# Two-part eviction straight from the banks, low parts and squares from GpSimd to VectorE, and tokens added in the banks, in a four-layer transformer on one core

## Chip, core and metric

The kernel runs on one core of a Trainium2 chip. A core has TensorE (PE, matmuls and transposes), VectorE (DVE), ScalarE (ACT), GpSimd (POOL) and SyncE (SP, which issues DMAs). Matmul results land in PSUM, eight banks of 128 partitions x 512 fp32; all else is in SBUF. The metric is the device time of one execution in microseconds (us), as the median over runs; lower is better. All times below are in us unless marked ns.

## The reference

256 tokens of width 1024 pass two blocks. The first block has two layers, each of a mixer, a feed-forward and a gated per-layer input:

```python
h = h + mix(_rms(h, norm_mix[i]))            # i=0: moba + dilated attention; i=1: compressed/selected/window attention (nsa)
h = h + _swiglu(_rms(h, norm_ffn[i]), w_ffn_gate[i], w_ffn_up[i], w_ffn_down[i])
gate = jax.nn.sigmoid(_rms(h, norm_ple[i]) @ w_ple_gate[i])
h = h + gate * (p[i] @ w_ple_proj[i])
```

The second block has two layers, each of a hybrid mixer (windowed attention beside a short convolution) and a mixture of 32 experts with two experts per token, and a last norm:

```python
x = x + hybrid_mixer(rmsnorm(x, norm_mix[l]), ...)
x = x + hierarchical_moe(rmsnorm(x, norm_ffn[l]), ...)
return rmsnorm(x, norm_final)
```

## The kernel before

**Numbers in two parts.** Most matrix products are made to fp32 accuracy from fp32r operands: an operand is cast to a high part, and its low part is the difference. `mm3` (L329 to L331) then issues three matmuls: high x high, low x high, high x low. In the first block and in the hybrid mixers, weights and activations are both split so. In the expert stages the weights go through TensorE unsplit.

**Weights.** SP loads weight blocks of 1 MB into a ring of SBUF buffers. `Split` turns them into parts, in the order of a job list: `make` casts the high part on ACT (L193) and puts the low part on a list, and `lows` issues the listed subtractions (L201) on `self.second`, which is DVE, but POOL during the per-layer gate (`ple`, L921) and at the transition into the second hybrid layer. `get(job)` casts what is needed, then as many further jobs as buffers allow (`pump`, unless `ahead` is false), then issues all the low parts, and hands out the job's parts. All engines work through their own queues in program order, so the place of a call in the program sets the order on ACT and DVE.

**Normalisation.** `Norm.half` squares half a token tile (ACT, with the sum accumulated), and POOL scales the first half's sum (L344). `norm` makes the reciprocal root (`rs`, DVE and ACT) and writes the normalised tile `xn` on DVE (L352). `turn(t)` transposes it by eight TensorE transposes of 128 x 128 (L366), four into each of two banks. Then, before the change, ACT scales bank 0's four chunks by the gain back into `xn` (L378), with a cast of two chunks into the high parts XH behind each pair (L373); DVE scales bank 1's four chunks (L382); ACT casts those in one instruction of 512 columns; DVE makes the low parts XL by three subtractions (L386). There are two token tiles, t = 0 and 1, and one turn for each before every stage.

**First block.** `last_steps` (L870) stands at the end of each mixer: the output projection's finish with the next norm, two products with the per-layer input's projection (`ple_product`, copied from their banks by ACT, L868), then `turn(0)` and `turn(1)` for the feed-forward, in an order written by hand in the list T1. `ffn` runs over 22 blocks of the hidden width: gate and up matmuls into one bank, silu on ACT (L903), product on DVE (L904), cast and difference (L905, L906), and the down matmuls of the block before. `ple` runs over two token tiles, two output halves and four weight blocks each; the sigmoid is L943, its product with the saved projection L946, the addition to the residual stream h L390; the next stage's `turn(0)` stands inside its second tile. The second layer's attention is planned by `Attention`, with the projections (`proj_steps`) stepped through beside it.

**Second block.** The hybrid mixers sum squares of their outputs in `halves`, with the additions on POOL (L1350). An expert layer runs over 16 pairs of experts; each pair's result is scattered back onto the tokens by matmuls (L1795) that accumulate in four banks `total` over all pairs. `Router.take` had replaced the tokens in h by a high and a low part; at the last pair, `join` (L1532) adds them into h again, on DVE and POOL, and `add_tiles` then adds the banks to h. After the first expert layer this is the transition into the second hybrid layer, where it is interleaved with weight casts; after the second, the tail: squares, reciprocal root, scaling by the final gain (L1863) and four output DMAs (L1864) from temporary buffers.

Of the kernel before, what the change touches and what calls it, by code (L numbers as in the profile page):

```python
# [153 lines left out]
class Split:  # L154


    def __init__(self, nc, ring, size):
        self.nc, self.ring, self.size = nc, ring, size
        self.jobs, self.at, self.made, self.free, self.low, self.pools = [], {}, {}, [], [], []
        self.second = nc.vector  # L160
        self.spare = 1

# [35 lines left out]
    def lows(self):  # L198

        for eng, vl, src, vh, key in self.low:  # L200
# [3 lines left out]
        self.low = []  # L204
# [56 lines left out]
def tile_kernel(ctx: ExitStack, tc: tile.TileContext, x, out, cat, sat, stop=None):  # L261
# [71 lines left out]
    class Norm:  # L333
# [12 lines left out]

        def norm(self, t):
# [13 lines left out]
        def turn(self, t, raw=False):  # L361
            src = h[:, t] if raw else self.xn[t]
            xn = tmp.tile([128, D], F32, name="xn", tag="xn") if raw else self.xn[t]
# [3 lines left out]

            to = [self.to[:, t, k] if self.low is None else xn[:, 128 * k:128 * k + 128] for k in range(8)]
            f_ = [slice(128 * c, 128 * c + 128) for c in range(4)]

            def parts(a, b):
                v = xn[:, 128 * a:128 * b].rearrange("p (c n) -> p c n", n=128)
                nc.scalar.copy(self.to[:, t, a:b], v)  # L373
                return self.low[:, t, a:b], v, self.to[:, t, a:b]

            lows = []
# [106 lines left out]
    with ExitStack() as c1:  # L483
# [83 lines left out]
        def proj(name, b, nq, pair=None, skew=None, mid=None, bank=acc, ahead=True):  # L567
# [30 lines left out]
            yield 0, o[0]  # L598
# [265 lines left out]
        def ple_product(i, b, pp, pv):  # L864

            for t, o in proj(f"pp{i}", b, 1, pp, bank=wps, ahead=False):
# [3 lines left out]
        def last_steps(i, outp, nxt, pp, pv):  # L870
            fns = [lambda: outp.finish(nxt, T1[10 + 6 * i]), lambda: ple_product(i, 0, pp, pv), lambda: ple_product(i, 1, pp, pv),
                   lambda: nxt.turn(0), lambda: nxt.turn(1)]
            for k in sorted(range(len(fns)), key=lambda k: T1[11 + 6 * i + k]):
                fns[k]()
# [46 lines left out]
        def ple(i, nm, pv, nxt):  # L921

            seq = [(b, q) for b in range(2) for q in range(4)]
            split.second = nc.gpsimd
# [24 lines left out]
            split.second = nc.vector  # L949
# [149 lines left out]
        def nsa(nm, nxt):  # L1099
# [142 lines left out]
            att.hold()  # L1242
            next(fill)
# [3 lines left out]
            att.run(AT1)  # L1247
            side.drain()
# [20 lines left out]
    with ExitStack() as c2:  # L1269
# [41 lines left out]
        def mixer(l, qkv, sq, yh, yl):  # L1311
# [31 lines left out]
            def halves(br, c, y, gain, n):  # L1343
# [166 lines left out]
        class Router:  # L1510
# [19 lines left out]
            def join(self, t, eng):  # L1530

                eng.tensor_add(self.tokens[:, t], self.high[:, t], self.low[:, t])  # L1532
# [147 lines left out]
        def moe(l, nm, rt, after, until):  # L1680
# [111 lines left out]
            def scatter(pr, ys, back, n):  # L1792
                for t in range(2):
# [29 lines left out]
            for pr in range(16):  # L1823
# [24 lines left out]
            for n in range(2):  # L1848
# [108 lines left out]
```

## Time and profile before

| | us |
|---|---|
| median of 3 runs | 1916.67 (1911.02 to 1917.64) |
| the profiled execution | 1910.32 |
| its span, first to last instruction | 1908.5 |
| TensorE / DVE / ACT / POOL busy | 1777.5 / 811.0 / 674.4 / 69.1 |
| mean granted TensorE clock, share of full | 0.974 |

The stages follow each other: first layer's mixer 0 to 141, feed-forward to 332, gate to 370, second layer's mixer to 534, feed-forward to 724, gate to 763, hybrid mixer to 862, experts to 1318, hybrid mixer to 1460, experts to 1897, tail to 1908.5. A duration in a row is that of one instruction or of the run of instructions that the row counts; instructions of one engine overlap a little at their ends, so that the distance of two starts is shorter than a duration. The bracket gives the engine's idle time just before, and what ended it.

### The profile page before, as it was taken

The numbers are of one execution on the slowest core, as the hardware profiler recorded it, in microseconds if no ns is written. First come the engines' busy times: TensorE is split into PE (matmuls) and PEld (weight loads), VectorE is DVE, ScalarE is ACT, GpSimd is POOL, SyncE is SP. The second block draws the span as 40 slices with busy tenths as digits, with TensorE's granted clock in tenths as the row PEclk, the third lists the DMA queues.
The fourth block names the chain that finished last, engine by engine and source line by source line (L and its number), as shares of the span: only waits on it lengthen the run. The fifth ranks groups of instructions, "written<-read, shape, count | busy, mean of one in ns | idle before, by whom it ended". The sixth has DMA issues, their size and how long they took to land. (4 is left out here: it accounts for less than half of the span.)

```text
span 1908.5 us, 25241 instructions
## 1 busy us (share of the span) xinstructions
PE 1777.5 (93%) x9983; PEld 1169.5 (61%) x9983; DVE 811.0 (42%) x1772; ACT 674.4 (35%) x1371; POOL 69.1 (4%) x92
## 2 busy tenths in 40 slices
PE   8998999898999999999999978997999999978996
PEld 6778999786689997874444443443874444433442
DVE  6667455767775556872111111113773111111112
ACT  6656445646574446651111110113552111110111
POOL 0000000300000003000000000001010000000000
PEclk9999999999999999999999989998998999998998
DMA  8437555442255554749999999999649999999996
GB/s 299 154 125 244 203 188 193 131 160 66 95 177 199 199 191 134 267 164 396 421 421 421 420 421 378 422 420 385 223 155 374 420 421 421 420 420 377 421 421 279
DMA packets 152908, 555.76 MB, mean 291 GB/s; under 512 B 9872, under 2 KB 69712, under 8 KB 103632
## 3 DMA queue, kind: packets, MB, share of 16 engines
q1 hardware_dynamic: 150672, 546.45, 73.9%
q0 software_dynamic: 2112, 7.63, 1.2%
q8 instruction: 81, 1.33, 0.3%
q14 instruction: 43, 0.35, 0.1%
HBM read 552.96 MB, written 1.09 MB: 290 GB/s over the span
## 5 line engine op out<-in xcount | busy, mean ns | idle before, releaser
L1745 PE MATMUL wps<-wring,h 128*64 128x512 f32 x1936 | 454.0, 596 | 10.6 <-DMA wring<-in_w_expert_up_dram 7.9
L1745 PEld LDWEIGHTS wps<-wring,h 128*64 128x64 f32 x1936 | 150.0, 138 | 287.3 <-issue 258.6
L201 DVE TENSOR_TENSOR wlo<-wring,whi 128x1024 fp32r<-128x1024 f32 (+1 forms) x273 | 288.3, 1094 | 73.6 <-ACT whi L193 73.3
L193 ACT CAST whi<-wring 128x1024 fp32r<-128x1024 f32 (+1 forms) x283 | 254.8, 945 | 23.0 <-PE acc L331 12.0
L329 PE MATMUL wps<-xh,whi 128*128 128x256 f32 x832 | 236.5, 284 | 4.7 <-ACT xh L373 4.7
L330 PE MATMUL wps<-xl,whi 128*128 128x256 f32 x832 | 234.8, 282 | 1.3 <-DVE xl L386 1.3
L331 PE MATMUL wps<-xh,wlo 128*128 128x256 f32 x832 | 234.5, 282 | 0.0
L1780 PE MATMUL wps<-wring,aT 128*64 128x512 f32 x984 | 227.4, 597 | 0.0
L1758 DVE SCALAR_TENSOR_TENSOR a<-wps,gs,a 128x256 f32<-128x256 f32 x64 | 28.0, 479 | 369.8 <-PE wps L1745 369.8
L329 PEld LDWEIGHTS wps<-xh,whi 128*128 128x128 f32 x832 | 157.5, 189 | 10.5 <-ACT xh L373 5.2
L1789 DVE SCALAR_TENSOR_TENSOR yl<-wps,gs,yh 128x512 fp32r<-128x512 f32 x64 | 47.9, 750 | 267.8 <-ACT yh L1788 263.9
L331 PEld LDWEIGHTS wps<-xh,wlo 128*128 128x128 f32 x832 | 160.3, 193 | 0.0
L330 PEld LDWEIGHTS wps<-xl,whi 128*128 128x128 f32 x832 | 157.5, 189 | 3.2 <-DVE xl L386 1.8
L329 PE MATMUL acc<-whi,xh 128*128 128x512 f32 (+1 forms) x360 | 146.6, 407 | 3.3 <-ACT whi L193 3.3
L1780 PEld LDWEIGHTS wps<-wring,aT 128*64 128x64 f32 x984 | 70.8, 137 | 128.4 <-issue 123.0
L331 PE MATMUL acc<-whi,xl 128*128 128x512 f32 (+1 forms) x360 | 141.3, 392 | 8.5 <-DVE xl L386 8.5
L330 PE MATMUL acc<-wlo,xh 128*128 128x512 f32 (+1 forms) x360 | 141.4, 393 | 2.3 <-DVE wlo L201 2.3
L1788 ACT ACTIVATE yh<-wps,gs 128x512 fp32r<-128x512 f32 x64 | 43.8, 687 | 262.9 <-PE wps L1780 212.2
L1769 ACT COPY aT<-wps 128x256 f32<-128x256 f32 x32 | 11.9, 372 | 239.7 <-PE wps L1768 239.7
L1755 ACT ACTIVATE a<-wps,gs 128x512 f32<-128x512 f32 x32 | 22.0, 688 | 179.9 <-PE wps L1745 179.9
L331 PEld LDWEIGHTS acc<-whi,xl 128*128 128x128 f32 x360 | 69.8, 194 | 24.9 <-DVE xl L386 10.2
L329 PEld LDWEIGHTS acc<-whi,xh 128*128 128x128 f32 x360 | 70.1, 195 | 18.1 <-ACT whi L193 4.6
(374 smaller groups left out, 2424.5 us busy)
## 6 DMA issues: line engine op xcount, KB each, us to landing
wring<-in_w_expert_down_dram SPq DMA_DIRECT2D x123, 1024.0 KB, 19.8
wring<-in_w_expert_up_dram SPq DMA_DIRECT2D x122, 1024.0 KB, 19.8
wring<-in_w_expert_gate_dram SPq DMA_DIRECT2D x120, 1024.0 KB, 19.8
wring<-in_w_ffn_gate_dram SPq DMA_DIRECT2D x22, 1024.0 KB, 9.1
wring<-in_w_ffn_up_dram SPq DMA_DIRECT2D x22, 1024.0 KB, 5.4
wring<-in_w_ffn_down_dram SPq DMA_DIRECT2D x22, 1024.0 KB, 7.4
wring<-in_w_in_dram SPq DMA_DIRECT2D x18, 1024.0 KB, 8.6
wring<-in_w_in_ab_dram SPq DMA_DIRECT2D x10, 1024.0 KB, 8.7
```

Source lines behind the costliest of these rows:

```text
L193: self.nc.scalar.copy(vh, src)
L201: eng.tensor_sub(vl, src, vh)
L329: nc.tensor.matmul(o, lh, rh, start=start, stop=False)
L330: nc.tensor.matmul(o, lh, rl, start=False, stop=False)
L331: nc.tensor.matmul(o, ll, rh, start=False, stop=stop)
L1745: nc.tensor.matmul(o[i][64 * ab:64 * ab + 64, :], xg[:, k, at:at + 64], ws[ab][:, c, :], start=k == 0, stop=k == 7)
L1755: nc.scalar.activation(a, o[0], AF.Silu, scale=r)
L1758: nc.vector.scalar_tensor_tensor(a[:, s_], o[1][:, s_], r, a[:, s_], ALU.mult, ALU.mult)
L1769: (nc.vector.tensor_copy if hf else nc.scalar.copy)(aT[:, 2 * hf:2 * hf + 2], pt[:, 256 * hf:256 * hf + 256].rearrange("p (j n) -> p j n", ...
L1780: nc.tensor.matmul(y[d2][64 * ab:64 * ab + 64, :], aT[:, 2 * hf + j, 64 * ab:64 * ab + 64], ws[ab][:, j, 512 * d2:512 * d2 + 512], start=h ...
L1788: nc.scalar.activation(ys[0][:, s_], y[d2], AF.Copy, scale=g)
L1789: nc.vector.scalar_tensor_tensor(ys[1][:, s_], y[d2], g, ys[0][:, s_], ALU.mult, ALU.subtract)
```

## The change

- `turn`: for each of the eight chunks, ACT scales it from its bank straight into the high part, and DVE makes the low part by one instruction that scales the same chunk of the same bank and subtracts the high part. The casts, the subtractions and the detour over `xn` go.
- `last_steps`: `turn(0)` moves between the two pieces of the last product.
- `ple` and the transition: low parts stay on DVE. The transition takes its tiles by `take`: squares from the banks, copies to h and the sum's offset on DVE, and only the first low part ahead of `turn(0)`.
- `Split.late`, set in the second attention: the low parts of jobs cast ahead are issued at the next `get`.
- `halves`: the additions of squares go to DVE.
- Experts: `join` goes; at pair 14, eight matmuls with an identity add the tokens' high and low parts in the banks.
- Tail: scatter by token tile, squares from the banks, gain product on DVE, last scaling half on ACT and half on DVE, output from h.

```diff
@@ class Split
     def make(self, spare=0):
...
+        if key not in self.ring.tiles:
+            self.lows()
...
-    def lows(self):
-
-        for eng, vl, src, vh, key in self.low:
+    def lows(self, n=None):
+
+        now, self.low = self.low[:n], [] if n is None else self.low[n:]
+        for eng, vl, src, vh, key in now:
             eng.tensor_sub(vl, src, vh)
...
     def get(self, job, ahead=True):
...
+        n = len(self.low) if self.late else None
         if ahead:
             self.pump()
-        self.lows()
+        self.lows(n)
@@ class Norm
+        def banks(self, t, v):
+
+            junk = tmp.tile([128, 512], BF16, name="junk", tag="junk", bufs=1)
+            s0, s1 = (small.tile([128, 1], F32, name="ss", tag=f"ss{t}{b}", bufs=2) for b in range(2))
+            for b, s in enumerate((s0, s1)):
+                nc.scalar.activation(junk, v[b], AF.Square, accum_out=s)
+            self.ss[t, 0], self.ss[t, 1] = s0, s1
+
+        def offset(self, t):
+            nc.vector.tensor_scalar(self.ss[t, 0], self.ss[t, 0], 1.0 / D, EPS, ALU.mult, ALU.add)
@@ def turn
-            for c in range(4):
-                nc.scalar.activation(to[c], pts[0][:, f_[c]], AF.Copy, scale=self.gain[:, c:c + 1])
-                if c % 2 and self.low is not None:
-                    lows.append(parts(c - 1, c + 1))
-            for c in range(4):
-                nc.vector.tensor_scalar(to[4 + c], pts[1][:, f_[c]], self.gain[:, 4 + c:5 + c], None, ALU.mult)
-            if self.low is not None:
-                lows.append(parts(4, 8))
-            for o, v, hi in lows:
-                nc.vector.tensor_sub(o, v, hi)
+            for c in range(8):
+                v = pts[c // 4][:, 128 * (c % 4):128 * (c % 4) + 128]
+                g, to = self.gain[:, c:c + 1], self.to[:, t, c]
+                if self.low is not None:
+                    nc.scalar.activation(to, v, AF.Copy, scale=g)
+                    nc.vector.scalar_tensor_tensor(self.low[:, t, c], v, g, to, ALU.mult, ALU.subtract)
...
@@ def proj
+                    if between and t == 0:
+                        yield 0, o[0]
+                        between()
@@ def last_steps
+            outp.finish(nxt, T1[10 + 6 * i])
+            ple_product(i, 1 - i, pp, pv)
+            ple_product(i, i, pp, pv, lambda: nxt.turn(0))
+            nxt.turn(1)
@@ def ple
-            split.second = nc.gpsimd
@@ second attention
+            split.late = True
             next(fill)
             for _ in att.start():
...
             att.run(AT1)
+            split.late = False
@@ def halves
-                    nc.gpsimd.tensor_add(sq[:, br], sq[:, br], s_)
+                    nc.vector.tensor_add(sq[:, br], sq[:, br], s_)
@@ experts
-                if pr == 15:
+                if pr == 14:
+
+                    idr = ptile([128, 128], F32R, "idr", bufs=1)
+                    nc.scalar.copy(idr, ident)
                     for t in range(2):
-                        rt.join(t, nc.gpsimd if t else nc.vector)
+                        for d2 in range(2):
+                            for part in (rt.high, rt.low):
+                                nc.tensor.matmul(total[t][d2], idr, part[:, t, :, 64 * d2:64 * d2 + 64].rearrange("p k q -> p q k"),
+                                                 start=False, stop=False, skip_group_check=True)
@@ tail
-            for n in range(2):
-                scatter(*last, n)
+            for t in range(2):
+                for n in range(2):
+                    scatter(*last, n, (t,))
...
+            for t in range(2):
+                after.banks(t, total[t])
             for t in range(2):
                 for b in range(2):
-                    add_half(t, b, total[t][b], after)
+                    nc.vector.tensor_mul(h[:, t, bs[b]], total[t][b], nf[:, bs[b]])
+                after.offset(t)
             for t in range(2):
                 r = rs(after.ss[t, 1], 1.0 / D, 1, bias=after.ss[t, 0])
-                for b in range(2):
-                    s_ = slice(512 * b, 512 * b + 512)
-                    o = tmp.tile([128, 512], F32, name="o", tag="xn")
-                    nc.vector.scalar_tensor_tensor(o, h[:, t, s_], r, nf[:, s_], ALU.mult, ALU.mult)
-                    nc.sync.dma_start(out[0, 128 * t:128 * t + 128, s_], o)
+                nc.scalar.activation(h[:, t, bs[0]], h[:, t, bs[0]], AF.Copy, scale=r)
+                nc.sync.dma_start(out[0, 128 * t:128 * t + 128, bs[0]], h[:, t, bs[0]])
+                nc.vector.tensor_scalar(h[:, t, bs[1]], h[:, t, bs[1]], r, None, ALU.mult)
+                nc.sync.dma_start(out[0, 128 * t:128 * t + 128, bs[1]], h[:, t, bs[1]])
@@ transition
-                            add_tiles((0,), total, nm)
-                            split2.second = nc.gpsimd
+                            def take(t):
+
+                                nm.banks(t, total[t])
+                                for b in range(2):
+                                    nc.vector.tensor_copy(h[:, t, 512 * b:512 * b + 512], total[t][b])
+                                nm.offset(t)
+                                nm.norm(t)
+
+                            take(0)
                             split2.pump(PUMP[0])
+                            split2.lows(1)
+                            nm.turn(0)
                             split2.lows()
-                            nm.turn(0)
                             split2.pump(PUMP[1])
                             split2.lows()
-                            add_tiles((1,), total, nm)
-                            split2.second = nc.vector
+                            take(1)
```

## Rows read from the trace of the kernel before

**Rows 1.** The page's busy time, share of the span and instructions per engine.

```profile
PE 1777.5 (93%) x9983; PEld 1169.5 (61%) x9983; DVE 811.0 (42%) x1772; ACT 674.4 (35%) x1371; POOL 69.1 (4%) x92
```

**Rows 2.** Stretches: length, each engine's busy time, granted clock, DMA share, GB/s.

```profile
141.00:332.00 191.00, 185.41 (x1335) 174.57 (x1334) 110.36 (x145) 96.77 (x140) 2.44 (x4) 1.00 0.61 207
...
862.00:1318.00 456.00, 427.07 (x2070) 187.40 (x2069) 73.08 (x163) 60.87 (x111) 2.40 (x1) 0.97 1.00 413
```

**Rows 3.** TensorE's timeline, 139 to 166: start, duration, line, [idle before <- ended by].

```profile
145.20 0.38 PE L329 MATMUL wps<-xh,whi 128*128 128x256 f32 x1 [2.34 <-ACT xh L373]
146.34 0.39 PE L330 MATMUL wps<-xl,whi 128*128 128x256 f32 x1 [0.75 <-DVE xl L386]
...
159.88 0.50 PE L329 MATMUL acc<-whi,ah 128*128 128x512 f32 x1 [2.50 <-ACT ah L905]
```

**Rows 4.** ACT's timeline of the same stretch.

```profile
141.64 0.63 ACT L378 ACTIVATE xn<-wps,sm 128x128 f32<-128x128 f32 x2
...
146.54 9.63 ACT L193 CAST whi<-wring 128x1024 fp32r<-128x1024 f32 x10
...
159.43 0.40 ACT L905 CAST ah<-a 128x256 fp32r<-128x256 f32 x1 [1.56 <-DVE a L904]
```

**Rows 5.** DVE's timeline of the same stretch.

```profile
147.62 11.44 DVE L201 TENSOR_TENSOR wlo<-wring,whi 128x1024 fp32r<-128x1024 f32 x10 [0.26 <-ACT whi L193]
158.98 0.41 DVE L904 TENSOR_TENSOR a<-sg,wps 128x256 f32<-128x256 f32 x1
```

**Rows 6.** Timelines: DVE and ACT at 381, TensorE at 884.

```profile
381.37 0.69 DVE L1069 COPY c2k<-wps 64x508 f32<-64x508 f32 x1 [1.06 <-ACT c2k L1067]
...
380.76 1.07 ACT L1067 COPY c2k<-wps 64x512 f32<-64x512 f32 x2 [1.70 <-PE wps L1065]
...
884.84 0.50 PE L1768 MATMUL wps<-idg,a 128*128 128x128 f32 x2 [0.46 <-ACT aT L1769]
```

**Rows 7.** Two DVE lines by form: duration min/median/max in ns, first and last start.

```profile
L1758 DVE SCALAR_TENSOR_TENSOR a<-wps,gs,a x64: 473/476/486, 883.3 to 1884.5; 128x256 f32<-128x256 f32 x64
...
L1789 DVE SCALAR_TENSOR_TENSOR yl<-wps,gs,yh x64: 741/751/752, 892.3 to 1895.0; 128x512 fp32r<-128x512 f32 x64
```

**Rows 8.** TensorE's timeline at the start.

```profile
9.50 0.80 PE L329 MATMUL acc<-whi,xh 128*128 128x512 f32 x1 [2.81 <-ACT whi L193]
```

**Rows 9.** Timelines of POOL, TensorE, ACT around the gate stages; DVE lines by form.

```profile
351.48 10.65 POOL L201 TENSOR_TENSOR wlo<-wring,whi 128x1024 fp32r<-128x1024 f32 x4 [4.18 <-DVE xn L352]
...
362.46 0.50 PE L331 MATMUL acc<-whi,xl 128*128 128x512 f32 x1 [3.20 <-DVE xl L386]
...
369.40 1.11 PE L366 MATMUL wps<-idg,xn 128*128 128x128 f32 x8 [1.40 <-DVE xn L352]
...
763.80 0.63 ACT L378 ACTIVATE xn<-wps,idg 128x128 f32<-128x128 f32 x2 [5.19 <-PE wps L366]
...
L946 DVE TENSOR_TENSOR sgp<-sgp,pv x8: 678/694/1874, 341.2 to 755.8; 128x512 f32<-128x512 f32 x8
...
L390 DVE TENSOR_TENSOR h<-h,sgp x8: 691/692/2776, 341.9 to 756.5; 128x512 f32<-128x512 f32 x8
...
L386 DVE TENSOR_TENSOR xl<-xn,xh x48: 411/425/2885, 7.8 to 1339.1; 128x256 fp32r<-128x256 f32 x32, 128x512 fp32r<-128x512 f32 x16
```

**Rows 10.** DVE's timeline in the second attention.

```profile
444.18 1.23 DVE L201 TENSOR_TENSOR wlo<-wring,whi 128x1024 fp32r<-128x1024 f32 x1 [2.10 <-ACT whi L193]
```

**Rows 11.** TensorE's timeline: strided matmuls, a wait for weights, last scatter.

```profile
384.71 3.66 PE L1076 MATMUL wps<-c2k,wring 128*128 128x80 f32 x25
...
1291.35 3.65 PE L1745 MATMUL wps<-wring,h 128*64 128x512 f32 x16 [1.33 <-DMA wring<-in_w_expert_gate_dram]
...
1316.83 1.10 PE L1795 MATMUL acc<-yl,back 128*128 128x512 f32 x4
```

**Rows 12.** Timelines: TensorE at the transition, DVE at the end.

```profile
1321.25 0.63 PE L366 MATMUL wps<-idg,xn 128*128 128x128 f32 x4 [3.32 <-DVE xn L352]
...
1904.01 1.42 DVE L1863 SCALAR_TENSOR_TENSOR o<-h,rs,X 128x512 f32<-128x512 f32 x2 [0.68 <-DMA out_dram<-o]
```

More of the change, by code (lines that the diff above doesn't have):

```diff
@@ L161, in __init__ @@
         self.spare = 1
+        self.late = False
     def add(self, job, key, view, last):
@@ L203, in lows @@
                 self.ring.done(key)
-        self.low = []
     def pump(self, most=99):
@@ L362, in turn @@
             src = h[:, t] if raw else self.xn[t]
-            xn = tmp.tile([128, D], F32, name="xn", tag="xn") if raw else self.xn[t]
             pts = [wps(), wps()]
@@ L366, in turn @@
                 nc.tensor.transpose(pts[k // 4][:, 128 * (k % 4):128 * (k % 4) + 128], src[:, 128 * k:128 * k + 128], ident)
[L368 to L376, printed above, removed]
-            for c in range(4):
-                nc.scalar.activation(to[c], pts[0][:, f_[c]], AF.Copy, scale=self.gain[:, c:c + 1])
-                if c % 2 and self.low is not None:
-                    lows.append(parts(c - 1, c + 1))
-            for c in range(4):
-                nc.vector.tensor_scalar(to[4 + c], pts[1][:, f_[c]], self.gain[:, 4 + c:5 + c], None, ALU.mult)
-            if self.low is not None:
-                lows.append(parts(4, 8))
-            for o, v, hi in lows:
-                nc.vector.tensor_sub(o, v, hi)
+            for c in range(8):
[4 more added lines that the diff above has]
+                    nc.vector.scalar_tensor_tensor(self.low[:, t, c], v, g, to, ALU.mult, ALU.subtract)
+                elif c < 4:
+                    nc.scalar.activation(to, v, AF.Copy, scale=g)
+                else:
+                    nc.vector.tensor_scalar(to, v, g, None, ALU.mult)
     def add_half(t, b, v, nxt):
@@ L564, in tile_kernel, with proj @@
             plan_moe(l)
-        def proj(name, b, nq, pair=None, skew=None, mid=None, bank=acc, ahead=True):
+        def proj(name, b, nq, pair=None, skew=None, mid=None, bank=acc, ahead=True, between=None):
             o = [bank(), bank()]
@@ L595, in proj @@
                     piece(q, t)
+                    if between and t == 0:
+                        yield 0, o[0]
+                        between()
                 split.done((name, b, q))
                 side.tick()
-            yield 0, o[0]
+            if not between:
+                yield 0, o[0]
             yield 1, o[1]
@@ L862, in ple_inputs, with ple_product @@
                 yield 0
-        def ple_product(i, b, pp, pv):
-            for t, o in proj(f"pp{i}", b, 1, pp, bank=wps, ahead=False):
+        def ple_product(i, b, pp, pv, between=None):
+            for t, o in proj(f"pp{i}", b, 1, pp, bank=wps, ahead=False, between=between):
                 pv[b, t] = keep.tile([128, 512], F32, name="pv", tag="pv", bufs=4)
@@ L870, in last_steps @@
         def last_steps(i, outp, nxt, pp, pv):
[L871 to L874, printed above, removed]
+            outp.finish(nxt, T1[10 + 6 * i])
+            ple_product(i, 1 - i, pp, pv)
+            ple_product(i, i, pp, pv, lambda: nxt.turn(0))
+            nxt.turn(1)
         def ffn(i, nm, nxt):
@@ L948, in ple @@
                 nxt.norm(t)
-            split.second = nc.vector
         rows_d = dram.tile([24, 383], F32, name="rows_d")
@@ L1528, in take @@
                     nc.scalar.copy(self.high[:, t, :, s_], self.tokens[:, t, :, s_])
-            def join(self, t, eng):
-                eng.tensor_add(self.tokens[:, t], self.high[:, t], self.low[:, t])
             def turn(self, t, hf):
@@ L1790, in down, with scatter @@
                 return ys
-            def scatter(pr, ys, back, n):
-                for t in range(2):
+            def scatter(pr, ys, back, n, ts=(0, 1)):
+                for t in ts:
                     for d2 in range(2):
```

6 lines of the change are left out of this document (4 added, 2 removed).

## The prediction

> **What bounds the kernel now.** I read the page's busy table first: TensorE is busy 93% of the span, VectorE (DVE) 42%, ScalarE (ACT) 35%, GpSimd (POOL) 4% [rows 1]. So 69 us of POOL work is not a bound by its size; what counts is who waits for it, and whom it slows. The stretches come next [rows 2]. In the feed-forward stretch TensorE is busy 185 of 191 us with DMA at 0.61: what is lost or won there moves everything behind it. In an expert stretch DMA is at 1.00: a TensorE microsecond there is free as long as it is smaller than a wait for weights. So every step is priced at the idle time of TensorE around it, outside the expert stretches.
>
> At the entry of a feed-forward stage, TensorE turns both token tiles in one run of transposes, waits 2.34 for the first high part and 0.75 for the first low part, and then 2.50 more before the first down matmul at 159.88 [rows 3]. Behind the turn, ACT makes ten casts from 146.54 on, and only then the silu [rows 4]; DVE makes the ten low parts, 1.14 us apart, and only then the product at 158.98 that the down matmul needs [rows 5]. So this wait counts from the moment when ACT is through with the turn.
>
> **The new eviction.** Before, ACT scales the four chunks of one bank while DVE scales the four of the other; casts and subtractions follow in SBUF. ACT starts at 141.64 [rows 4] and, by two turns in the 4.9 us up to 146.54, needs some 2.5 a turn. After, ACT and DVE read each chunk from the same bank, one behind the other. Does ACT's next chunk wait for DVE's read? The trace of before has few pairs to ask. On the bank at 380.76, ACT copies partitions 0 to 63 and DVE partitions 64 to 127, with no data in common; DVE starts at 381.37, after 1.06 of waiting for ACT [rows 6]. TensorE, too, waits 0.46 to write one half of a bank until ACT has read the other half [rows 6]. No two engines' accesses to one bank overlap anywhere that I looked. I take it that the two readers alternate.
>
> The Trainium skill ("PSUM — Partial Sum Buffer", section "PSUM bank collisions raise a hardware error") asks for exactly this guard between engines, two readers included, in a bank and its 32-partition quadrant; by it the time is that of this forecast, and without it that of the first rival below. The trace goes further than the page, since its two readers had different quadrants and one waited all the same.
>
> One chunk then takes ACT's 0.37 (two in a row span 0.63 [rows 4]), a hand-over of some 0.04 (DVE's 158.98 plus 0.41 [rows 5], to ACT's cast of that product at 159.43 [rows 4]), DVE's read and a hand-over back. DVE's instruction is bounded below by ACT's pace for a plain scaling of the same columns, 0.31 [rows 4], and above by DVE's own two-tensor form at 256 columns, 0.476; that form at 512 columns takes 0.751 [rows 7], so a column costs 1.07 ns and 128 of them 0.34, which I take. The cycle is 0.79 (0.92 at the upper end). Eight cycles, less one overlap of some 0.4 where the bank changes, keep ACT for 5.4 instead of 2.5: **2.8 us more of ACT per turn** (2.2 to 4).
>
> **Part by part,** against the profiled execution's 1910.3:
>
> Start: the first cast of a weight stands behind the turn on ACT, and TensorE's first matmul waits 2.81 for that cast, until 9.50 [rows 8]. +2.9, the turn and a hand-over (-0.4 if the readers overlap, +4 at the slow cycle).
>
> Feed-forward entries: two, of one pattern. Turn 0 moves between two pieces of the last projection and starts some 1.2 earlier, at 140.4; two turns then take 2 x 5.4 and a copy of 0.6 between them, so the ten casts start near 152.0 instead of 146.54. The casts, ten low parts and the product shift rigidly. TensorE does not catch that up: it would finish the second gate and up blocks near 162 and wait until 165.3 instead of 159.88. +5.4 each, +10.8 (gain of 0.75 each if nothing serialises; 7 each at the upper cycle).
>
> Low parts of the per-layer gate (two stages): POOL's four in a row take 10.65, and beside them a DVE multiply takes 1.87 where the median is 0.69, an add 2.78 where it is 0.69, and a subtraction of the turn 2.89 where the wide ones take some 0.7 [rows 9]. So 5.5 us of DVE time come back when POOL is empty, against five low parts of 1.14 [rows 5], 5.7, that DVE now makes: even. What decides is ACT, whose sigmoid for the last half stands behind the serial turn. That turn ends 2.8 later by itself, and by some 2.1 more because a turn earlier in the stage was late by 2.8 and waited 0.7 less for TensorE; behind it, multiply, add and normalisation get 1.8 back from the empty POOL. So the last transposes, which TensorE waits 1.40 for before 369.40 [rows 9], come 3.0 later: +3.0. In the second layer ACT idles 5.19 before the turn there [rows 9]; less the normalisation and the transposes, some 2 in all, 3 of it is cover, of a chain that is 4.6 later, since its earlier turns are later too: +1.5. Ends: -4.3 and -5.8 if readers overlap (TensorE's wait of 3.20 at 362.46 for a subtraction beside POOL [rows 9] and its like of 3.86 in the second layer go, with some 1.1 and 1.9 of matmuls stretched behind them), +5 and +4 at the slow cycle.
>
> Delayed low parts in the second attention: three of them, like the one at 444.18 that makes DVE idle 2.10 [rows 10] with the score work of the attention queued behind it. DVE gets to that work earlier; what waits next is the cast itself. 4.85 us of DVE idle time, about half of it on the path: -2.5 (0 to -4).
>
> Squares of the other mixer: 12 additions of 256 columns leave POOL for DVE, where 256 columns take 0.41 [rows 5], so 2.5 a layer. They lie beside attention matmuls in stretches where DVE has room, and only the last pair is near the path; without the cover 0.8 a layer. 0 (-1 to +1).
>
> Tokens added in the banks: eight more matmuls of 512 columns per expert layer. Four contiguous ones last 1.10 in a row [rows 11], the last with its full length, so some 0.235 apart; 8 of them make 1.9. Their moving operand steps by 512 bytes. Of strides, the trace has 80 columns at 64 bytes, twenty-five matmuls in 3.66, 0.146 each [rows 11], and transposes at 8 bytes, 128 columns each in some 0.24 [rows 6]; the latter, carried to 512 columns, would make 0.96 each and 7.7 in all, the upper end. I take 1.9, since the row with the longer stride is the nearer. TensorE waits 1.33 for weights there, one of three such waits [rows 11], 3.9 in all, which hides 1.9 and not 7.7. 0; if the cover were gone, +1.9 a layer. The join of POOL and DVE that goes was waited for by nobody before the stage's end.
>
> The Trainium skill ("SBUF — State Buffer", section "Door 1: The DMA port swizzle") says that each access which crosses into a new 16-byte line pays a penalty; every element would do so here. By it the eight would lie toward their upper end and the sum come to the 1940 of the last rival; the row at 64 bytes, which crosses a line at each element too, does not show it.
>
> Transition: TensorE idles 3.32 before the transposes of 1321.25 [rows 12]. DVE's add (0.69 [rows 9]) no longer stands ahead of the squares, and no POOL runs beside the normalisation, about 0.9 by the slow forms of rows 9: -1.6. The turn costs 2.8, and DVE now makes four low parts of half size, 0.6 each, around it, some of which the weights' first use waits for: +0.8. +2.0 (-2 to +4).
>
> Tail: the wait of 0.68 for an output buffer goes, and ACT takes one of the last two scalings, 0.71 [rows 12]; a tile's offset no longer goes through POOL, 0.3. The load of the final gain is issued on SP ahead of the last scatter instead of behind it, with no output queued there yet. -1.7 (-0.7 to -2.1).
>
> Sum: 2.9 + 10.8 + 3.0 + 1.5 - 2.5 + 2.0 - 1.7 = **+16.0**, 1926.3 for an execution like the profiled one. The median of the runs shown is 6.4 above that execution; on it I predict **1932**.
>
> **Rivals.** *The readers overlap.* Then a turn takes 2.9 and ACT and DVE are both freed by the casts and subtractions. For it: every data dependence of the new form allows it. Against: rows 6. Terms: -0.4 at the start, -1.5 at the feed-forward entries, -1.4 at the gate stages' entries, -4.3 and -5.8 behind them, -2.5, -2.0, -2.1: -20.0, 1897. It decides at once, in every turn.
>
> *They alternate, but the cost is covered.* A projection takes a chunk in three matmuls of 0.235, 0.7, nearly the pace of 0.79, and its first low part comes after 0.8 instead of 1.8. If the ten casts weren't what the down matmul waits for, the entries would cost 2 each and the gate stages nothing: 2.9 + 4 - 2.5 - 1.7 = +2.7, 1919. Against: the order of rows 4 and 5.
>
> *The strided matmuls are slow.* 7.7 less a cover of 3.9, twice, on top of the forecast: +7.6, 1940. Against: the row at 64 bytes.
>
> **How the numbers follow.** Forecast 0.58, overlap 0.20, covered 0.16, slow strides 0.06. About 0.5% (9.6 us) is what a measurement of this kernel tells from no change. Overlap is faster; covered is mostly the same, with 0.03 faster; of the forecast 0.03 falls within 0.5%. Faster 0.23, same 0.16, slower 0.61. The forecast's own range is 1921 to 1944, which takes in all but the outermost of the ends above; reaching down over the covered case to 1905 leaves out the overlap alone, 2 in 10.
>
> **What would show it.** Right: ACT's scalings 0.79 apart with DVE's reads between them; the ten casts at the feed-forward entry starting about 10 us after TensorE's first transpose there, and an idle TensorE of over 4 us before the first down matmul; POOL nearly empty. Wrong: scalings 0.31 apart with DVE one chunk behind; casts at the old distance; the eight strided matmuls longer than 3.9; no DVE idle time saved in the second attention.

## The result and the profile after

| | before | changed |
|---|---|---|
| median, us | 1913.85 (1910.89 to 1917.64, 4 runs) | 1933.74 (1929.30 to 1934.18, 4 runs) |
| the profiled execution, us | 1910.32 | 1934.18 |
| span, us | 1908.5 | 1932.4 |

The ratio of the changed kernel to the one before is 1.0103, with a 95% interval of 1.0086 to 1.0121: slower by 1.0%, 19.9 us between the medians and 23.9 between the profiled executions. 1932 was forecast.

The page's busy table of the changed kernel, as in [rows 1]:

```profile
PE 1795.9 (93%) x9999; PEld 1179.8 (61%) x9999; DVE 810.0 (42%) x1814; ACT 679.1 (35%) x1391; POOL 21.4 (1%) x60
```

POOL is nearly empty, as was meant, and ACT and DVE are as busy as before. The loss is in their waits. Two rows of the changed kernel's view of waits (who waited for whom: us in total, times, longest):

```profile
DVE xl L386 <- ACT xh L385: 50.8, 101, 6.2
...
ACT xh L385 <- DVE xl L386: 47.3, 96, 1.7
```

L385 and L386 are the two halves of the new eviction. DVE's wait for ACT's high part is a data dependence. ACT's wait for DVE has no data in it: ACT's next chunk has nothing to do with the low part that DVE makes. 96 times are six in each of the 16 turns, one for each pair of neighbouring chunks that share a bank; 47.3 over 16 turns is 2.96 a turn.

The entry of the first feed-forward, ACT's timeline of the changed kernel (start, duration, what, idle before), answers to [rows 4]:

```profile
145.44 0.37 ACT L385 ACTIVATE xh<-wps,sm 128x128 fp32r<-128x128 f32 x1 [0.46 <-DVE xl L386]
146.23 0.37 ACT L385 ACTIVATE xh<-wps,sm 128x128 fp32r<-128x128 f32 x1 [0.42 <-DVE xl L386]
147.02 0.63 ACT L385 ACTIVATE xh<-wps,sm 128x128 fp32r<-128x128 f32 x2 [0.42 <-DVE xl L386]
...
155.64 9.59 ACT L196 CAST whi<-wring 128x1024 fp32r<-128x1024 f32 x10
```

The scalings stand 0.79 apart, with one pair 0.26 apart where the bank changes (the row with x2). The ten casts begin at 155.64. DVE and TensorE of the same stretch answer to [rows 5] and [rows 3]:

```profile
146.63 0.35 DVE L386 SCALAR_TENSOR_TENSOR xl<-wps,sm,xh 128x128 fp32r<-128x128 f32 x1 [0.44 <-ACT xh L385]
...
156.70 11.44 DVE L205 TENSOR_TENSOR wlo<-wring,whi 128x1024 fp32r<-128x1024 f32 x10 [0.58 <-ACT whi L196]
168.06 0.41 DVE L912 TENSOR_TENSOR a<-sg,wps 128x256 f32<-128x256 f32 x1
```

```profile
147.83 0.66 PE L380 MATMUL wps<-idg,xn 128*128 128x128 f32 x4 [1.02 <-DVE xl L386]
150.81 0.38 PE L333 MATMUL wps<-xh,whi 128*128 128x256 f32 x1 [2.32 <-ACT xh L385]
157.98 0.38 PE L335 MATMUL wps<-xh,wlo 128*128 128x256 f32 x1 [0.76 <-DVE wlo L205]
168.97 0.80 PE L333 MATMUL acc<-whi,ah 128*128 128x512 f32 x1 [2.76 <-ACT ah L913]
```

The first down matmul stands at 168.97 instead of 159.88. Even the transposes of the second tile are late: they wait 1.02 for DVE to leave a bank.

**Where it is lost.** The table says by how much a matmul of TensorE starts later than the same matmul (the n-th of its source line) of the kernel before, as the median over the matmuls of a stretch, from the two timelines. The columns after the first are experiments, told below. Times of the stretches are those of the kernel before.

| stretch | changed | e12 order alone | e2 old turn | e3 new turn alone | e1 alternate | e5 few casts |
|---|---|---|---|---|---|---|
| first projection, 24 to 29 | 2.7 | 0.3 | 0.1 | 2.6 | 0.9 | 2.7 |
| first attention's end, 115 to 128 | 4.4 | 1.8 | 0.0 | 4.2 | 2.4 | 4.6 |
| feed-forward, 200 to 300 | 10.7 | 1.6 | -0.9 | 9.8 | 4.0 | 6.3 |
| second attention, 385 to 425 | 15.3 | -2.5 | -3.3 | 18.0 | 2.9 | 10.7 |
| its end, 500 to 525 | 16.0 | -4.4 | -4.1 | 20.9 | 2.1 | 11.3 |
| feed-forward, 600 to 700 | 23.2 | -4.7 | -5.1 | 27.9 | 2.2 | 12.8 |
| hybrid mixer, 775 to 800 | 27.5 | -11.5 | -10.7 | 34.9 | -2.1 | 15.6 |
| experts, 1000 to 1050 | 27.1 | -13.3 | -11.3 | 36.6 | -3.8 | 16.4 |
| experts' end, 1300 to 1308 | 27.2 | -12.9 | -10.9 | 36.4 | -3.7 | 16.3 |
| hybrid mixer, 1400 to 1430 | 26.2 | -13.2 | -12.1 | 37.8 | -1.8 | 17.2 |
| experts, 1600 to 1650 | 25.3 | -15.4 | -13.1 | 37.8 | -3.0 | 16.0 |
| span | 23.9 | -16.5 | -14.7 | 37.4 | -4.4 | 14.7 |

The changed kernel loses at the two feed-forward entries (6.3 and 7.2) and at the gate stages with what follows them (4.7 and 4.3), gains nothing net in the second attention and nothing in the experts, gets 1.9 back from the first experts' end to the second experts, and 1.5 at the tail. One column is one execution. Stretches with the same code differ by 1 to 1.5 between columns, where a stretch of TensorE at the lower of its two clock levels fell elsewhere, so a difference of one stretch under 1.5 is not read here. In the second attention, where no turn stands, the spread is wider still: from 385 to 525, e10 (below) falls back by 2.3 and e12 gains 1.9, with granted clocks of 0.94 and 0.98 from 405 to 512.

### The profile page after: what moved, and what is told of

It is laid out like the page before. It is cut to its first block, busy times and chain, and to the rows that moved or that the text cites. A ratio compares the mean times of both kernels' runs of the same rounds, so it can differ in the third digit from the quotient of the medians.

```text
span 1932.4 us, 25272 instructions
## 1 busy us (share of the span) xinstructions
PE 1795.9 (93%) x9999; PEld 1179.8 (61%) x9999; DVE 810.0 (42%) x1814; ACT 679.1 (35%) x1391; POOL 21.4 (1%) x60
## 5 line engine op out<-in xcount | busy, mean ns | idle before, releaser
L205 DVE TENSOR_TENSOR wlo<-wring,whi 128x1024 fp32r<-128x1024 f32 (+1 forms) x283 | 299.5, 1097 | 66.5 <-ACT whi L196 66.0
```

The lines of the kernel that those rows point to most:

```text
L205: eng.tensor_sub(vl, src, vh)
```

## The experiments

The changed kernel is altered, unless the kernel before is named. The kernel before ran beside each; its medians were 1910.48 to 1911.89.

### e1: neighbouring chunks in different banks

```diff
-            for k in range(8):
-                nc.tensor.transpose(pts[k // 4][:, 128 * (k % 4):128 * (k % 4) + 128], src[:, 128 * k:128 * k + 128], ident)
+            for k in (0, 2, 4, 6, 1, 3, 5, 7):
+                nc.tensor.transpose(pts[k % 2][:, 128 * (k // 2):128 * (k // 2) + 128], src[:, 128 * k:128 * k + 128], ident)
             for c in range(8):
-                v = pts[c // 4][:, 128 * (c % 4):128 * (c % 4) + 128]
+                v = pts[c % 2][:, 128 * (c // 2):128 * (c // 2) + 128]
```

> The changed kernel with neighbouring chunks of a turn in different banks: even chunks transposed into the first bank, odd ones into the second, everything else the same, the number of instructions included. Theory A (two readers of one bank take turns, readers of different banks do not): ACT scales chunk c+1 while DVE reads chunk c, so two chunks take what one took, and eight of ACT's scalings end after some 3.2 us instead of 5.4; the casts at the feed-forward entry begin some 5 us earlier, and the time falls by 18 to 26, to 1908 to 1916. Theory B (the many small instructions, each with its hand-over, set the pace, whatever the bank): the scalings stay 0.79 apart and the time stays at 1929 to 1936.

1902.69, ratio 0.9947 (0.9929 to 0.9965) to the kernel before: 31 below the changed kernel by the medians and 1.6% by the two ratios, more than theory A asked for. ACT's timeline at the start of the program:

```profile
6.65 0.62 ACT L385 ACTIVATE xh<-wps,sm 128x128 fp32r<-128x128 f32 x2 [0.49 <-PE wps L380]
7.44 0.62 ACT L385 ACTIVATE xh<-wps,sm 128x128 fp32r<-128x128 f32 x2 [0.16 <-DVE xl L386]
8.22 0.62 ACT L385 ACTIVATE xh<-wps,sm 128x128 fp32r<-128x128 f32 x2 [0.16 <-DVE xl L386]
9.01 0.37 ACT L385 ACTIVATE xh<-wps,sm 128x128 fp32r<-128x128 f32 x1 [0.16 <-DVE xl L386]
```

The cycle of 0.79 is the same, but two chunks fit into it. The same instructions, each with its data hand-over, run at twice the pace when neighbours lie in different banks; theory B falls.

### e2: the eviction of before in the changed kernel

```diff
-            for c in range(8):
-                v = pts[c // 4][:, 128 * (c % 4):128 * (c % 4) + 128]
...
+            for c in range(4):
+                nc.scalar.activation(to[c], pts[0][:, f_[c]], AF.Copy, scale=self.gain[:, c:c + 1])
...
+            for o, v, hi in lows:
+                nc.vector.tensor_sub(o, v, hi)
```

> The changed kernel with the eviction of the kernel before (scalings, casts and subtractions, two banks on two engines); all other parts of the change stay. Theory A (the eviction is the whole loss and the rest of the change is a small gain): 1903 to 1912, at or under the kernel before, with the gate stages shorter than before since POOL no longer slows DVE. Theory B (low parts on DVE and the other parts cost as well): 1918 or more.

1896.12, ratio 0.9919 (0.9897 to 0.9941): 37.6 below the changed kernel by the medians, 1.8% by the two ratios, and 14 below the kernel before. The rest of the change is a gain, and larger than theory A had it. The table puts 2.4 and 5.6 of it at the gate stages. Why there, DVE's timeline shows, first of this kernel, then of the kernel before:

```profile
350.99 3.49 DVE L205 TENSOR_TENSOR wlo<-wring,whi 128x1024 fp32r<-128x1024 f32 x3
354.40 0.68 DVE L964 TENSOR_TENSOR sgp<-sgp,pv 128x512 f32<-128x512 f32 x1
355.11 0.69 DVE L405 TENSOR_TENSOR h<-h,sgp 128x512 f32<-128x512 f32 x1
```

```profile
355.23 1.87 DVE L946 TENSOR_TENSOR sgp<-sgp,pv 128x512 f32<-128x512 f32 x1 [3.30 <-ACT sgp L943]
357.14 2.78 DVE L390 TENSOR_TENSOR h<-h,sgp 128x512 f32<-128x512 f32 x1
```

Three of the low parts that DVE took over fill the 3.30 in which it had waited for the sigmoid, and multiply and add are back at 0.69.

### e3: the new eviction alone, in the kernel before

The body of `turn` of the changed kernel, put into the kernel before; all else as before.

> The kernel before with the new eviction alone. Theory A (the eviction costs 2.7 of ACT per turn, unhidden at the start and at both feed-forward entries, partly at the gate stages, where POOL still slows DVE): 18 to 30 above the kernel before, 1932 to 1944. Theory B (it costs only together with the other parts, since these fill DVE): within 8 of the kernel before.

1947.97, ratio 1.0186 (1.0162 to 1.0210): 37.5 above the kernel before, over theory A's range, and 1.9% against the 1.8% that e2 gets by taking it out. It costs 8.2 and 7.0 from a feed-forward to the mixer behind it. TensorE before the last transposes there, to be held against the 1.40 of [rows 9]:

```profile
385.11 1.11 PE L365 MATMUL wps<-idg,xn 128*128 128x128 f32 x4 [6.20 <-DVE xn L352]
```

### e4 and e9: without the delayed low parts

```diff
-            split.late = True
...
-            split.late = False
```

e4 is the changed kernel without these lines, e9 the kernel of e2 without them.

> The changed kernel without the delayed low parts in the second attention. Theory A (the delay gains 3.4 at the first score work and gives most of it back to stretches at the lower clock behind it): from the start of that attention to its end the stretch of some 165 us differs by less than 1.5 from that of the changed kernel, while the score matmuls of the first blocks wait some 3 us for DVE again. Theory B (the delay is a plain gain that other losses of this stretch hide): that stretch is 2.5 to 4 longer than with the delay.

> The kernel of e2_old_turn without the delayed low parts in the second attention, so that the delay is seen with the eviction of before. Theory A (its early gain is mostly given back): the attention's stretch, from 385 to 525 of the kernel before, is 0 to 1.5 longer than with the delay. Theory B (a plain gain of 2.5): 2 to 3.5 longer.

One run each, 1929.42 and 1901.07; the first lies inside the changed kernel's own range, the second 5 above e2's median. From 385 to 525, e4's matmuls fall back by 1.9 and the changed kernel's by 0.7, a difference of 1.2; e9's fall back by 1.5 and e2's gain 0.8, a difference of 2.3. TensorE's wait for the score work of e2, then of e9:

```profile
441.87 1.47 PE L693 MATMUL wps<-kwT,qT 64*128 64x256 f32 x8 [1.20 <-DVE m L709]
```

```profile
445.34 2.20 PE L693 MATMUL wps<-kwT,qT 64*128 64x256 f32 x8 [3.28 <-DVE m L709]
```

2.1 of wait goes, as 2.1 goes in the changed kernel (1.20 instead of 3.31). So the delay does what it was meant to do at this wait. What is left of it at the end of the stretch is less sure. With the old eviction the pair speaks for theory B. With the new one, e5, e7 and e8 have the changed kernel's code in this stretch and move by +0.6, -0.8 and -0.8, where the changed kernel moves by +0.7, so that against e4's 1.9 the delay is worth anything from 1.2 to 2.6. The granted clock does not decide it: from 405 to 512 it was 0.95 in e4 and in the changed kernel, 0.97 in e5, 0.98 in e7 and e8. The delay is a gain in each of these pairs; that it is as much as 2.5 with the new eviction is not shown.

### e5 and e6: fewer casts at the feed-forward entry

```diff
             for c, wn in enumerate(("gate", "up")):
-                vh, vl = split.get((wn, i, j))
+                if j < 4:
+                    split.pump(2)
+                vh, vl = split.get((wn, i, j), j > 3)
```

> The changed kernel with the casts at a feed-forward entry spread out: each of the first twelve requests casts two jobs ahead instead of all that fit, so that some four casts and low parts stand before the first silu instead of ten. Theory A (the ten casts and low parts behind the slow turn are what the first down matmul waits for): its wait of 2.76 falls under 0.5 and each entry is 2 to 3 shorter, 4 to 6 in all, 1927 to 1931. Theory B (the entry is lost while TensorE follows the chunks of the turn, and would wait for weights' low parts anyway): within 2 of the changed kernel, or slower since casts come late for the third block.

> The kernel of e2_old_turn with the same spread casts. Theory A: its waits of 2.42 and 1.37 before the first down matmuls go, 2 to 4 in all, 1892 to 1894. Theory B: no gain, 1895 to 1898.

e5: 1925.63, ratio 1.0071 (1.0049 to 1.0094), 8 below the changed kernel. ACT's timeline of e5:

```profile
155.86 3.88 ACT L196 CAST whi<-wring 128x1024 fp32r<-128x1024 f32 x4
159.76 1.28 ACT L913 ACT_TABLE_LOAD   x1
161.06 0.39 ACT L913 ACTIVATE sg<-wps 128x256 f32<-128x256 f32 x1
```

Four casts instead of ten, and TensorE no longer waits for the first down matmul. The entries lose 1.7 and 1.5 (4.6 to 6.3, 11.3 to 12.8) instead of 6.3 and 7.2. They are 4.6 and 5.7 shorter, twice what theory A had: after a wait of 2.76 the changed kernel's matmul at 168.97 also took 0.80, where 0.50 followed the wait before, and its granted clock from 130 to 180 was 0.93 against e5's 0.97. So casts and low parts behind the turn carried most of an entry's loss. e6: 1893.74, ratio 0.9908 (0.9884 to 0.9932), which its interval does not tell from e2's.

### e7 and e8: what the token matmuls cost

```diff
-                                nc.tensor.matmul(total[t][d2], idr, part[:, t, :, 64 * d2:64 * d2 + 64].rearrange("p k q -> p q k"),
+                                nc.tensor.matmul(total[t][d2], idr, part[:, t].rearrange("p k q -> p (k q)")[:, 512 * d2:512 * d2 + 512],
```

```diff
-                    nc.scalar.copy(idr, ident)
+                    nc.scalar.mul(idr, ident, 0.5)
...
-                            for part in (rt.high, rt.low):
+                            for part in (rt.high, rt.low, rt.high, rt.low):
```

> The changed kernel whose eight matmuls per expert layer that add the tokens read 512 neighbouring columns instead of 512 columns that lie 512 bytes apart; the tokens are then added in another order than they should be. Theory A (the stride costs TensorE time): their distance falls from 0.486 to about 0.235 each, 2.0 per layer, and the total stays, since the waits for weights behind them grow by as much. Theory B (the distance of 0.486 comes from elsewhere, such as the loading of the stationary side): it stays at 0.486.

> The changed kernel with the token matmuls made twice with half an identity, sixteen per layer, 7.8 instead of 3.9. Theory A (three waits for weights of 1.3 each are all the cover there is): 3.9 per layer come on top, and the stretch from the middle of the first expert layer to its end is 3 to 4 longer, as in the second. Theory B (transfers run ahead far enough to hide more): no difference over 1.

The changed kernel's TensorE timeline, then e7's:

```profile
1306.82 0.69 PE L1854 MATMUL acc<-low,idr 128*128 128x512 f32 x1
1307.31 0.69 PE L1854 MATMUL acc<-high,idr 128*128 128x512 f32 x1
...
1328.51 3.65 PE L1750 MATMUL wps<-wring,h 128*64 128x512 f32 x14 [0.88 <-DMA wring<-in_w_expert_up_dram]
```

```profile
1303.51 0.40 PE L1854 MATMUL acc<-low,idr 128*128 128x512 f32 x1
1303.74 0.39 PE L1854 MATMUL acc<-high,idr 128*128 128x512 f32 x1
...
1321.34 3.65 PE L1750 MATMUL wps<-wring,h 128*64 128x512 f32 x16 [1.30 <-DMA wring<-in_w_expert_up_dram]
```

The stride of 512 bytes costs: 0.49 apart with it, 0.23 without, so eight make 3.9. With them two of the three waits for weights of [rows 11] are gone and one of 0.88 is left; with contiguous columns two of 1.3 stand. e7's time, 1931.87 in a single run, is within the changed kernel's range.

e8 came to 1938.08 in a single run. What its sixteen token matmuls cost has to be read beside them: against the kernel before, TensorE is 24.6 late in the middle of the first experts (1000 to 1050), 26.0 just ahead of the token matmuls (1270 to 1278), 33.9 just behind them, and 28.1 near the end of the layer (1308 to 1316). In the second layer it is 27.1 ahead of them and 29.2 at the end. So 2.1 of the 7.8 is left in each layer, and the other 1.4 and 1.2 of these stretches (24.6 to 26.0, 25.9 to 27.1) came before the token matmuls began. That is between the theories: some 5.7 of the 7.8 are hidden, more than the three waits of 3.9 make, but not all. What hides more than these waits stays open.

### e10, e11 and e12: a bank at a time

```diff
-            for c in range(8):
...
-                    nc.scalar.activation(to, v, AF.Copy, scale=g)
-                    nc.vector.scalar_tensor_tensor(self.low[:, t, c], v, g, to, ALU.mult, ALU.subtract)
...
+            for c in range(on_act):
+                nc.scalar.activation(to[c], v[c], AF.Copy, scale=g[c])
+            for c in range(on_act, 8):
+                nc.vector.tensor_scalar(to[c], v[c], g[c], None, ALU.mult)
+            if self.low is not None:
+                for c in range(8):
+                    nc.vector.scalar_tensor_tensor(self.low[:, t, c], v[c], g[c], to[c], ALU.mult, ALU.subtract)
```

`on_act` is 4 in e10 and 8 in e11 and e12. e10 and e11 have e5's spread casts too; e12 has the changed kernel's.

> The changed kernel with spread casts (as e5_few_casts) and an eviction that hands over whole banks: ACT scales the first bank's four chunks into the high parts while DVE does so with the second bank's, then DVE makes all eight low parts straight from the banks. The same sixteen reads of the banks as in the changed kernel, with two hand-overs per turn instead of sixteen. Theory A (the alternation on one bank is the loss): ACT is through with a turn after 1.3, DVE after some 3.8, and the time falls from the 1926 of e5_few_casts to 1885 to 1896. Theory B (sixteen reads of banks cost in any order): 1905 or more.

> As e10_bank_by_bank_four, with all eight high parts on ACT: it does the second bank while DVE makes the low parts of the first. Theory A: ACT is through after 2.5, DVE after some 3.9; 1889 to 1898, above e10_bank_by_bank_four by up to 1.2 at each place where ACT holds TensorE up, 1 to 6 in all. Theory B: 1905 or more.

> The changed kernel with one thing altered: the same sixteen instructions of a turn in another order, first ACT's eight scalings into the high parts, then DVE's eight low parts, so that DVE reads the first bank while ACT reads the second and a bank changes hands once. Theory A (the alternation on one bank is the loss of the change): ACT ends a turn after 2.2 as in e11_bank_by_bank_eight, and the whole loss goes: 1888 to 1898, 34 to 46 below the changed kernel. Theory B (a good part of the gain of e11_bank_by_bank_eight came from the spread casts): 1900 or more.

e10 came to 1895.93, ratio 0.9917 (0.9896 to 0.9939); e11 to 1890.52, ratio 0.9897 (0.9874 to 0.9919); e12 to 1894.05, ratio 0.9907 (0.9882 to 0.9932). e12 has instruction for instruction the eviction of the changed kernel, in another order, and is 39.7 below it by the medians, 2.0% by the two ratios. ACT's and DVE's timelines of e12 at the entry of the feed-forward:

```profile
142.03 2.18 ACT L386 ACTIVATE xh<-wps,sm 128x128 fp32r<-128x128 f32 x8
...
144.51 2.26 ACT L386 ACTIVATE xh<-wps,sm 128x128 fp32r<-128x128 f32 x8
146.52 9.76 ACT L196 CAST whi<-wring 128x1024 fp32r<-128x1024 f32 x10
```

```profile
143.21 2.16 DVE L391 SCALAR_TENSOR_TENSOR xl<-wps,sm,xh 128x128 fp32r<-128x128 f32 x8 [0.65 <-ACT xh L386]
145.77 2.16 DVE L391 SCALAR_TENSOR_TENSOR xl<-wps,sm,xh 128x128 fp32r<-128x128 f32 x8 [0.40 <-ACT xh L386]
```

A turn takes each engine some 2.2 instead of 5.3 (144.61 to 149.91 on ACT in the changed kernel), and the casts start at 146.52, where they started before the change. ACT's wait for DVE, 47.3 in the changed kernel, has no row at all in e12's view of waits. This settles the cause: not the sixteen reads, not the instructions' size and not the data between them, but the order in which two engines take turns on a bank. The waits are seen by the semaphores that end them; whether the chip itself would bear two readers of one bank at once, no run here asks.

e10 against e11 went the other way than expected: giving DVE four of the high parts did not gain. Its median is 5 higher, but the two intervals overlap (0.9896 to 0.9919), so that the two kernels are not told apart. At the start, ACT is through early but then waits for the weights:

```profile
5.74 1.14 ACT L386 ACTIVATE xh<-wps,sm 128x128 fp32r<-128x128 f32 x4 [3.72 <-PE wps L380]
7.85 1.04 ACT L196 CAST whi<-wring 128x1024 fp32r<-128x1024 f32 x1 [0.97 <-DMA wring<-in_w_in_ab_dram]
```

DVE, with twelve instructions in a turn, then starts the weights' low parts later (9.70 instead of 9.08 in e11). That DVE is what counts in the other turns too was not tried apart.

e11 and e12 beat both kernels of the change, at 1.0% and 0.9% under the one before. But so do e2 and e6 with the old eviction, at 0.8% and 0.9%. With the same casts, e12 (0.9907) and e2 (0.9919) are not told apart, nor e11 (0.9897) and e6 (0.9908). So the eviction straight from the banks, in the right order, is shown to lose nothing; that it gains anything over the old one is not shown. What these kernels gain over the one before comes with the other parts of the change.

## Why the prediction was right, point by point

The time and the sign were right: 1932 against 1933.74, by the mechanism that had the highest chance. The terms, against the changed kernel's column:

| term | forecast | measured |
|---|---|---|
| start | +2.9 | +2.7 |
| first attention | not named | +1.7 |
| feed-forward entries | +5.4, +5.4 | +6.3, +7.2 |
| gate stages | +3.0, +1.5 | +4.7, +4.3 |
| second attention | -2.5 | +0.7 |
| squares, token sums in the experts | 0 | -0.4, +0.1 |
| transition and the mixer behind it | +2.0 | -1.9 |
| second experts, tail | 0, -1.7 | +0.1, -1.5 |
| sum | +16.0 | +23.9 |

The sum was 8 short between profiled executions, and the total came closer than that for a reason outside it: the profiled execution of before stood 6.4 under the median known then, but the medians of both kernels, in the comparison, are only 19.9 apart. That 1932 lies within 2 of the result is luck; the sum itself had two thirds of the loss.

**The cycle on a bank** was right to the hundredth: 0.79 forecast from three rows, 0.79 measured. That the two readers alternate rested on one row of before, DVE's 1.06 at 381.37 [rows 6], and e1 and e12 show it. The first rival, overlap, falls.

**The entries** were right in mechanism and 0.9 to 1.8 short. The casts started later than 152.0, at 155.64, since everything before had shifted by 4.4. TensorE itself was 4.4 later by the end of the first gate and up matmuls than at the entry (8.8 at 153 to 157 of the kernel before); so the last wait was 2.76, little more than the 2.50 of before, and not the over 4 that was named as a sign (the sum's own times, 162 and 165.3, make 3.3). At the first down matmul, 9.1 late, the first entry had cost 4.7. The rest of its 6.3 stands behind the wait and is not in the sum: the matmuls there ran 0.43 apart instead of 0.23, at a granted clock of 0.50, the lower level, from 169 to 172, where the kernel before had 1.00. e5 shows that the ten casts and low parts are what is waited for.

**The gate stages** are the terms that were most out: 9.0 against my 4.5. In the first stage 2.7 of the 4.7 stood at the last transposes, where the sum had 3.0. TensorE of the changed kernel, to be held against the 1.40 and the 1.11 of [rows 9]:

```profile
382.77 1.97 PE L380 MATMUL wps<-idg,xn 128*128 128x128 f32 x8 [6.26 <-DVE xn L367]
```

The 2.0 behind that wait are not in the sum: the transposes took 1.97 instead of 1.11, and the matmuls behind them ran 0.43 apart up to 387, at a granted clock of 0.50 from 382.7 to 385, where the kernel before had 1.00. And 2.7 was near 3.0 by two errors that cancel: the turns alone cost 5.9 at these transposes (e3), where I had 4.9, and the rest of the change gave back 3.2 (5.9 less 2.7), where I had 1.8. "Even" for DVE was wrong: in the first stage the low parts cost next to nothing, since DVE idled 3.30 just there, a wait that I had not set against them; with the old eviction the two stages gain 2.4 and 5.6 (e2). In the second stage e2 and e3 would add up to a loss of 1.4, which is what I had, but the changed kernel loses 4.3; e4, e5, e7 and e8, with the same code, lose 2.7, 2.8, 4.2 and 4.4. What keeps the two from adding up there stays open.

**The second attention**: the wait that the delay was aimed at went by 2.1, and at the end of the stretch 1.2 to 2.6 of it is left, against 2.5 forecast. The +0.7 of the changed kernel's column is one execution at a granted clock of 0.95; e7 and e8 gain 0.8 with the same code at 0.98.

**The token matmuls** hid, as forecast, though they took 3.9, where I had 1.9: as much as the three waits that I had for cover. By e8 some 5.7 can be hidden. The last rival, 7.7 of them with a part of it paid, falls too. The row at 64 bytes, which I took for the nearest, had been the wrong neighbour. The Trainium skill ("SBUF — State Buffer", section "Door 1: The DMA port swizzle") has a penalty for each access that crosses into a new 16-byte line. The trace agrees at 512 bytes: e7 shows a factor of 2.1. I had read the row at 64 bytes [rows 11] as showing none, and it doesn't show that: its 80 columns take 0.146 each, as long as a transpose of 128 neighbouring columns (eight in 1.11 [rows 9]). No run has that product with neighbouring columns.

**The transition** with the mixer behind it was forecast as a loss of 2.0 and came out as a gain of 1.9: up to the second experts the turn costs 1.4 in e3, where I had 2.8, and the other parts gain 2.2 in e2, where I had 0.8. The tail gave 1.5 of 1.7. At both, the squares straight from the banks make DVE wait, which I had not counted, though I had applied the same rule to the turn. DVE at the transition of the changed kernel:

```profile
1345.23 1.41 DVE L1911 COPY h<-acc 128x512 f32<-128x512 f32 x2 [1.25 <-ACT junk L356]
```

The copy of a bank waits for ACT's square of the same bank.

**The covered rival** falls too: it had 1919, and in e3 the turns' price of 37.5 is nearly three quarters of what ACT waits for DVE there, so most of it was paid. The row of e3's view of waits:

```profile
ACT xh L370 <- DVE xl L371: 51.7, 96, 3.8
```

## What to carry to other kernels

When two engines have to read the same banks, hand over whole banks: let one run through a bank while the other is in the next, and write the program in that order. Chunk by chunk on one bank, two readers run one after the other however independent their data are; in the view of waits this looks like an engine waiting for a result that it does not use. Then hold the mended form against the old one, too: here the new eviction, once in the right order, was not shown to beat it. And when work is moved onto an engine, look for the idle time in front of the instruction that it would push: a move that is "even" by sums can be free, as it was in the first gate stage.

## What the runs showed of the hardware

- On 128 columns from a bank to SBUF, ACT and DVE each take some 0.27 per instruction in a run of eight (2.16 to 2.26 for eight in e12), against 0.35 to 0.37 for one alone and 0.79 for a pair that alternates.
- A matmul of 512 columns takes 0.49 instead of 0.23 when neighbouring columns of its moving operand lie 512 bytes apart (e7).
- DVE's multiply and add next to POOL's subtractions took 1.87 and 2.78 instead of 0.69; with POOL empty all eight multiplies of the changed kernel take 0.68 to 0.70:

```profile
L953 DVE TENSOR_TENSOR sgp<-sgp,pv x8: 680/692/695, 354.3 to 785.1; 128x512 f32<-128x512 f32 x8
```
